# Two transformer blocks on one core: where the differences of the block products are made, the step of residual and norm in out1, and the places and order of down's first loads

## The chip, the core and the metric

One core of a Trainium2 chip runs the whole program. Its engines take their own instruction streams in order and wait for one another by semaphores: TensorE (PE in the views; its weight loads are PEld) multiplies into PSUM banks, VectorE (DVE), ScalarE (ACT) and GpSimd (POOL) work on SBUF, and all but POOL read PSUM; SyncE (SP) issues the transfers. The metric is the device time of one execution in microseconds.

## The reference, cut to what matters

Two blocks on 1024 tokens of width 1024, in float32. The first mixes by a gated recurrence and a stick-breaking attention, the second by two kinds of attention; both end in a gated feed-forward net of 2816 columns and a gate from a per-layer input.

```python
# first block
mix = concatenate([rmsnorm(o_hg, hg_out_norm) * silu(hg), o_sb]) @ w_out
h = h + rmsnorm(mix, attn_post_norm)
u = rmsnorm(h, ffn_pre_norm)
gate, up = split(u @ w_gate_up)
y = (silu(gate) * up) @ w_down
# second block
x = x + y_attention @ w_out
x = x + conv_ffn(rms_norm(x, ffn_norm_g), w_gate, w_up, conv_w, conv_b, w_down)
```

## The kernel before

The program is written with tiles and pools; the framework places the pools and plans the order in which each engine takes its instructions, so that a step may run ahead of one that the code writes before it, if its operands and its place are there. A pool's tiles lie at the address where the pool was opened, one pool behind the other (pools with `side="right"` from the other end), and a tile at an address that an older tile had waits until that one is read for the last time.

**Precision.** Each float32 operand is split into a high part, cast on ScalarE (L219), and a low part, the difference, on VectorE or POOL (L225); a product is three matmuls, high by high, high by low, low by high (`mm3`, L294 to L296; in the block products L1194 to L1196). A token tile is 128 tokens; there are 8.

**Stages around the change.** `out1` (first block) and `out2` (second) make the attention's output per token tile, add the residual, norm, and hand the tile `u_tok` to `put_uT`. `gate_up(s)` then multiplies by the gate's and up's weights, and `down(s)` by those of `w_down`; s is 0 in the first block and 1 in the second.

**out1.** Per tile i, `prep(i)` loads `o`, `gate` and `o_sb`, norms `o` (`norm_u`: square sum on ScalarE, a root in small steps, one step on VectorE, L549) and multiplies by the gate on POOL (L1018); the result is transposed on TensorE. `mm(i, c)` makes the two halves of the output. `fin(i)` norms `y` (L549), adds the residual on POOL (L1044), stores it as `h1` (L1045), and norms again into `u_tok` (square sum, root, L549). Its transposes (L1087) follow behind `mm(i+2)`. `x_res` and `u_tok` share the two buffers of `o_wk`.

**Block products.** `gate_up` uses seven products in place of eight, over a split of weights and tokens in two by two blocks. Tokens: even tiles are the first column of blocks, odd ones the second (`put_uT`: t = i % 2). Products 1 and 2 take B11 and B21, whose parts are made as the even tiles come. The other five take T2 = B22 - T1 (product 6), T1 = B12 - B11 (5), B22 - B12 (7), B21 - T2 (4) and B22 (3), and `right_operands` makes these once all tiles are there, in two halves of 256 columns: differences on POOL and VectorE (L1101), high parts on ScalarE, low ones on VectorE. Their tiles are q-tiles of 8 KB per partition: 8 in `q1` (B blocks and parts of 1 and 2; later those of 4 and one of 3), 7 in `q2`.

**Weights.** `add_pair` loads two raw weight tiles, `raw` and `raw2`, per chain (a 128-column piece of gate or up) and makes four units: the first directly, the second from sums on POOL (L141 to L144, in the one tile `s12`), the third and fourth from what these leave. Four split tiles `w` are live; `pump()` splits the next ones as far as tiles and raw tiles go. The two places of `raw2` are opened in `gate_up`, behind `q2`, so before it the units stop at the first sum.

**The order of products** is `sevens(s, chains)`: for s = 0 products go in pairs of chains 0 and 1; for s = 1 chain 0 goes first with chain 1 pushed in. From chain 2 on products 4 and 3 of a chain come behind product 1 of the next, in both.

**down.** `load(f)` loads a row tile of `act` (L1230) and splits it; `out` adds two rows' products into `y` (L1247). For s = 1 `y` starts as `h3`, loaded in `block1` (L592) ahead of `down`. `act` (4 tiles) is opened ahead of `act_raw` (2 of 4 KB), both from the address where `q1` began.

## Time and profile before

| | us |
|---|---|
| three runs | 2973.06, 2977.28, 2980.13 |
| median | 2977.28 |
| profiled execution | 2983.0 |
| its span, first to last instruction | 2981.2 |
| mean granted clock of TensorE in it | 0.978 of full |

The trace is of the one profiled execution. Busy shares are of the span. "Idle before" is how long an engine had stood still ahead of an instruction and what ended it. A merged line (x3) counts several instructions from the first one's start to the last one's end. The granted clock of a stretch says how far TensorE's clock was at the lower one of its two levels, 1.2 and 2.4 GHz.

### The profile page before, as it was taken

To read this page: it belongs to the slowest core of one execution; us is meant where nothing else is said; L and a number is where in the kernel's file an instruction comes from. 1 tells how busy PE (TensorE), PEld (TensorE's weight loads), DVE (VectorE), ACT (ScalarE), POOL (GpSimd) and SP (SyncE) were. 2 spreads that over 40 slices of the span, in tenths; PEclk is the share of its full clock that TensorE was granted. 3 is DMA by queue.
4 is the path that set the end of the run, shared out by engine and by line. 5 is a ranking of instruction groups with operands and counts; after the bars stand their busy time and mean duration, and the time that the engine had idled before them with its cause. 6 is when DMAs were issued, how large, how long until landed. Compare 5 with 4: busy or idle time off the path is not lost. (4 is left out here: it accounts for less than half of the span.)

```text
span 2981.2 us, 37288 instructions
## 1 busy us (share of the span) xinstructions
PE 2797.0 (94%) x13699; PEld 2295.8 (77%) x13699; DVE 1757.5 (59%) x3120; ACT 1168.8 (39%) x2237; POOL 721.9 (24%) x606
## 2 busy tenths in 40 slices
PE   8989988887999999999999999889979999799999
PEld 6878776765788887887788788767768888588877
DVE  4444687756433333557469775778775555455561
ACT  4121566644333334112246455656443333221131
POOL 1223000035433331222214100020163343122201
PEclk9989999998999999999999999999999999899999
DMA  4212545341322223322235865753322222433221
GB/s 131 67 45 97 156 132 141 116 138 64 92 81 79 83 80 146 106 85 92 69 112 161 215 154 175 198 135 78 124 64 85 81 83 85 158 99 106 75 76 47
DMA packets 277942, 321.36 MB, mean 108 GB/s; under 512 B 14646, under 2 KB 207194, under 8 KB 276222
## 3 DMA queue, kind: packets, MB, share of 16 engines
q1 hardware_dynamic: 277758, 318.97, 35.3%
q8 instruction: 108, 1.77, 0.2%
q14 instruction: 76, 0.62, 0.1%
HBM read 228.69 MB, written 92.59 MB: 108 GB/s over the span
## 5 line engine op out<-in xcount | busy, mean ns | idle before, releaser
L1194 PE MATMUL bank<-q,w 128*128 128x512 f32 x1232 | 484.5, 394 | 32.3 <-ACT w L219 25.5
L1195 PE MATMUL bank<-q,w 128*128 128x512 f32 x1232 | 483.1, 392 | 0.2 <-DVE q L225 0.2
L1196 PE MATMUL bank<-q,w 128*128 128x512 f32 x1232 | 482.1, 392 | 0.0
L219 ACT CAST w<-raw 128x1024 fp32r<-128x1024 f32 (+2 forms) x246 | 236.6, 971 | 532.5 <-DVE y L1247 285.7
L225 DVE TENSOR_TENSOR w<-raw,w 128x1024 fp32r<-128x1024 f32 (+2 forms) x242 | 312.4, 1300 | 134.1 <-ACT w L219 133.3
L1247 DVE TENSOR_TENSOR y<-y,bank 128x512 f32<-128x512 f32 x336 | 227.1, 686 | 171.4 <-PE bank L296 171.3
L294 PE MATMUL bank<-w,act 128*128 128x512 f32 x704 | 276.7, 393 | 26.3 <-ACT act L219 26.3
L1194 PEld LDWEIGHTS bank<-q,w 128*128 128x128 f32 x1232 | 233.7, 190 | 85.0 <-ACT w L219 27.0
L294 PE MATMUL bank<-w,u 128*128 128x512 f32 (+1 forms) x672 | 272.9, 406 | 6.5 <-ACT u L287 3.7
L295 PE MATMUL bank<-w,act 128*128 128x512 f32 x704 | 276.2, 392 | 0.0
L296 PE MATMUL bank<-w,act 128*128 128x512 f32 x704 | 275.8, 392 | 0.1
L1195 PEld LDWEIGHTS bank<-q,w 128*128 128x128 f32 x1232 | 233.3, 189 | 49.3 <-DVE q L225 0.6
L1196 PEld LDWEIGHTS bank<-q,w 128*128 128x128 f32 x1232 | 233.2, 189 | 49.2 <-DVE w L225 0.3
L295 PE MATMUL bank<-w,u 128*128 128x512 f32 (+1 forms) x672 | 266.4, 396 | 2.2 <-POOL w L225 2.0
L296 PE MATMUL bank<-w,u 128*128 128x512 f32 (+1 forms) x672 | 267.6, 398 | 0.0
L225 POOL TENSOR_TENSOR act<-act_raw,act 128x1024 fp32r<-128x1024 f32 x40 | 103.8, 2615 | 332.3 <-ACT act L219 332.3
L294 PEld LDWEIGHTS bank<-w,act 128*128 128x128 f32 x704 | 133.8, 190 | 55.0 <-ACT act L219 27.2
L1134 ACT COPY s<-bank 128x512 f32<-128x512 f32 x132 | 77.4, 588 | 200.7 <-PE bank L1196 200.7
L296 PEld LDWEIGHTS bank<-w,act 128*128 128x128 f32 x704 | 133.2, 189 | 29.2 <-DVE act L225 1.5
L295 PEld LDWEIGHTS bank<-w,act 128*128 128x128 f32 x704 | 133.6, 190 | 27.8
L294 PEld LDWEIGHTS bank<-w,u 128*128 128x128 f32 x672 | 128.0, 191 | 29.7 <-ACT u L287 4.7
L295 PEld LDWEIGHTS bank<-w,u 128*128 128x128 f32 x672 | 128.0, 190 | 25.1 <-POOL w L225 2.9
(360 smaller groups left out, 5571.1 us busy)
## 6 DMA issues: line engine op xcount, KB each, us to landing
raw<-in_w_gate_up_dram SPq DMA_DIRECT2D x44, 512.0 KB
act<-o SPq DMA_DIRECT2D x88, 256.0 KB
raw<-in_w_down_dram SPq DMA_DIRECT2D x44, 512.0 KB
act_raw<-act SPq DMA_DIRECT2D x44, 512.0 KB
raw<-in_w_in_dram SPq DMA_DIRECT2D x40, 512.0 KB
qk<-qkT SPq DMA_DIRECT2D x32, 384.0 KB
raw<-in_w_gate_dram SPq DMA_DIRECT2D x22, 512.0 KB
raw<-in_w_up_dram SPq DMA_DIRECT2D x22, 512.0 KB
```

The lines of the kernel that those rows point to most:

```text
L219: nc.scalar.copy(hi, src)
L225: e.tensor_tensor(lo, src, hi.bitcast(F32), ALU.subtract)
L294: mm(ps, lh, rh, start=start, stop=False)
L295: mm(ps, lh, rl, start=False, stop=False)
L296: mm(ps, ll, rh, start=False, stop=stop)
L1134: nc.scalar.copy(t, src)
L1194: nc.tensor.matmul(ps, w[:, 0, o], uh[:, k, :], start=first_mm, stop=False, skip_group_check=True)
L1195: nc.tensor.matmul(ps, w[:, 0, o], ul[:, k, :], start=False, stop=False, skip_group_check=True)
L1196: nc.tensor.matmul(ps, w[:, 1, o], uh[:, k, :], start=False, stop=k == 3, skip_group_check=True)
L1247: nc.vector.tensor_tensor(y, y, ps, ALU.add)
```

## The change

- **out1**: the gate times `o`, and `y` times its gain (`z`), are made on POOL from what is there before the norm; one VectorE step then multiplies by the root and the other factor, or multiplies and adds the residual. `o_wk` has three buffers.
- **Token differences**: `put_uT` makes T1 from PSUM when an odd tile comes, and B22 - B12 on POOL; for s = 1 also T2 from PSUM, its parts, and B21 - T2 (`behind`). For s = 0 `gate_up` makes T2's in a piece of three pairs and one of one. `right_operands` is left with splits.
- **Places**: for s = 1 T2 and its parts have a pool `q2n`, opened ahead of `out2`, and products 5 and 7 get the places of `out2`'s eight `y` tiles, joined in twos, whose pool now stays open. For s = 0 `raw2` and `s12` lie between two parts of the old `q2`.
- **Weights' sums**: `raw2` and `s12` are opened ahead of `out2` for s = 1, and behind four q-tiles for s = 0.
- **Order**: in `sevens(1)` product 2 of chain 1 comes ahead of product 6 of chain 0, its evacuation behind product 3. In chains 0 and 1 the twelve matmuls of a product go high by high, low by high, high by low.
- **down**: `act_raw` is opened ahead of `act`; the eight loads of `y` are issued behind the first two rows' loads.

```diff
@@ -57,7 +57,7 @@
...
     else:
-        seq = [(0, 1), (0, 2), (1, 1), (0, 6), (0, 5), (0, 7), (0, 4), (0, 3), (1, 2), (1, 6), (1, 5), (1, 7)]
+        seq = [(0, 1), (1, 1), (0, 2), (1, 2), (0, 6), (0, 5), (0, 7), (0, 4), (0, 3), (1, 6), (1, 5), (1, 7)]
         late = [(1, 4), (1, 3)]
@@ -577,19 +577,23 @@
...
         with ExitStack() as cq:
+            yp = self.yp = self.pool("y2", 1, ctx=cq, side="right")
             with ExitStack() as c1:
-                yp = self.pool("y2", 1, ctx=c1, side="right")
-                self.y = [yp.tile([P, D], F32, tag=f"y{i}", name=f"yy{i}") for i in range(NT)]
+                yy = [yp.tile([P, 2 * D], F32, tag=f"y{n}", name=f"yy{n}") for n in range(NT // 2)]
+                self.y = [yy[i // 2][:, (i % 2) * D:(i % 2 + 1) * D] for i in range(NT)]
+                del yy
                 wk = self.pool("t_wk", 2, ctx=c1, side="right")
...
                 self.q1 = self.pool("q1b", 8, ctx=cq)
+                self.qn = self.pool("q2n", 3, ctx=cq)
+                self.open_sums(cq, 1)
                 self.out2(wk)
+                self.y = None
             self.gate_up(1, cq)
...
             self.open_y(c1, 1)
-            for i in range(NT):
-                ld(out=self.y[i], in_=S["h3"][i * P:(i + 1) * P, :])
             self.down(1)
@@ -997,7 +1001,7 @@
...
             Y, OT = {}, {}
-            wk = self.pool("o_wk", 2, ctx=c)
+            wk = self.pool("o_wk", 3, ctx=c)
             gp = self.pool("o_g", 1, ctx=c)
@@ -1014,8 +1018,9 @@
...
                 ld(out=sb, in_=S["osbT"][:, i * P:(i + 1) * P].rearrange("(k p) t -> p k t", p=P))
-                self.norm_u(o, g_hg, o, 512, root=True)
-                nc.gpsimd.tensor_tensor(o, o, gt, ALU.mult)
+                r = self.rstd_sqrt(self.square_sum(o, 512), 512)
+                nc.gpsimd.tensor_tensor(gt, o, gt, ALU.mult)
+                nc.vector.scalar_tensor_tensor(out=o, in0=gt, scalar=r, in1=g_hg, op0=ALU.mult, op1=ALU.mult)
                 OT[i] = u = op.tile([P, 2, 8, P], F32R, tag="oT", name="oT")
@@ -1040,8 +1045,10 @@
...
                 ld(out=x, in_=A["x"][0, i * P:(i + 1) * P, :])
-                self.norm_u(y, g_post, y, root=True)
-                nc.gpsimd.tensor_tensor(y, y, x, ALU.add)
+                z = wk.tile([P, D], F32, tag="u", name="y_g")
+                nc.gpsimd.tensor_tensor(z, y, g_post, ALU.mult)
+                r = self.rstd_sqrt(self.square_sum(y, D), D)
+                nc.vector.scalar_tensor_tensor(out=y, in0=z, scalar=r, in1=x, op0=ALU.mult, op1=ALU.add)
                 ld(out=S["h1"][i * P:(i + 1) * P, :], in_=y)
@@ -1072,10 +1079,31 @@
-    def new_uT(self):
+    def new_uT(self, new=None):
...
         self.uT = {(k, t): self.q(q) for t in range(2) for k in range(2)}
+        self.T2 = None
+        if new is not None:
+            self.new_T2(new)
+    def new_T2(self, new):
+        self.T2 = self.q(new)
+        self.ub[6] = (self.q(new, F32R), self.q(new, F32R))
+    def sub(self, e, out, a, b, c):
+        e.tensor_tensor(out[:, :, c], a[:, :, c], b[:, :, c], ALU.subtract)
+    def behind(self, c, e=None):
+        nc = self.nc
+        if e is not None:
+            self.sub(e, self.T2, self.uT[1, 1], self.uT[0, 0], c)
+        hi, lo = self.ub[6]
+        self.split(hi[:, :, c], lo[:, :, c], self.T2[:, :, c], "act", "dve")
+        self.sub(nc.gpsimd, self.uT[1, 0], self.uT[1, 0], self.T2, c)
@@ -1086,43 +1114,54 @@
...
+            u = self.uT[k, t][:, :, c]
...
-                nc.vector.tensor_copy(self.uT[k, t][:, :, c], v)
+                nc.vector.tensor_copy(u, v)
...
-                nc.scalar.copy(self.uT[k, t][:, :, c], v)
...
-    def right_operands(self, q2):
-        nc = self.nc
-        B11, B12, B21, B22 = (self.uT[n] for n in ((0, 0), (0, 1), (1, 0), (1, 1)))
-        T2 = self.q(q2)
-        sub = lambda e, out, a, b: (lambda c: e.tensor_tensor(out[:, :, c], a[:, :, c], b[:, :, c], ALU.subtract))
-        pool, dve = nc.gpsimd, nc.vector
...
-        for n, pools, value, steps in (
-                (6, (q2, q2), T2, [sub(pool, B11, B12, B11), sub(dve, T2, B22, B11)]),
-                (5, (q2, q2), B11, []),
-                (7, (q2, q2), B12, [sub(pool, B12, B22, B12)]),
-                (4, (self.q1, self.q1), B21, [sub(pool, B21, B21, T2)]),
-                (3, (q2, self.q1), B22, [])):
-            hi, lo = self.ub[n] = tuple(self.q(p, F32R) for p in pools)
+                T1 = self.uT[0, 0][:, :, c]
+                if k == 0:
+                    nc.vector.tensor_tensor(T1, v, T1, ALU.subtract)
+                elif self.T2 is not None:
+                    nc.vector.tensor_tensor(self.T2[:, :, c], v, T1, ALU.subtract)
+                nc.scalar.copy(u, v)
+        if t == 1:
+            if self.T2 is not None:
+                self.behind(c)
+            self.sub(nc.gpsimd, self.uT[0, 1], self.uT[1, 1], self.uT[0, 1], c)
...
+    def right_operands(self, tiles):
...
+        for n, pools, value in ((5, tiles[0:2], (0, 0)), (7, tiles[2:4], (0, 1)),
+                                (4, [self.q1, self.q1], (1, 0)), (3, [tiles[4], self.q1], (1, 1))):
+            hi, lo = self.ub[n] = tuple(p() if callable(p) else self.q(p, F32R) for p in pools)
...
-                for f in steps:
-                    f(c)
-                self.split(hi[:, :, c], lo[:, :, c], value[:, :, c], "act", "dve")
+                self.split(hi[:, :, c], lo[:, :, c], self.uT[value][:, :, c], "act", "dve")
...
+    def open_sums(self, ctx, s):
+        self.W.open_raw("raw2", 2, ctx)
+        self.xp = self.pool(f"s12_{s}", 1, ctx=ctx)
...
-        q2 = self.pool(f"q2_{s}", 7, ctx=ctx)
-        self.W.open_raw("raw2", 2, ctx)
-        self.xp = self.pool(f"s12_{s}", 1, ctx=ctx)
+        if s == 0:
...
+            qa = self.pool("q2a", 4, ctx=ctx)
+            self.open_sums(ctx, s)
+            qb = self.pool("q2b", 3, ctx=ctx)
+            self.W.pump()
+            self.new_T2(qa)
+            for c in (slice(0, 384), slice(384, 512)):
+                self.behind(c, nc.vector)
+            tiles = [qa, qb, qb, qb, qa]
+        else:
+            tiles = [(lambda n=n: self.yp.tile([P, 4, 512], F32R, tag=f"y{n}", name="q")) for n in range(4)] + [self.qn]
...
-        self.W.pump()
-        self.right_operands(q2)
+        self.right_operands(tiles)
@@ -1188,19 +1227,25 @@
...
             w, (uh, ul) = self.W.get(U["p", s, c][unit]), self.ub[n]
-            for k in range(4):
+            parts = [(k, a, b) for k in range(4) for a, b in ((0, 0), (0, 1), (1, 0))]
+            if c < 2:
+                parts = [(k, a, b) for a, b in ((0, 0), (1, 0), (0, 1)) for k in range(4)]
+            for n_mm, (k, a, b) in enumerate(parts):
                 o = slice(half * 512 + k * P, half * 512 + (k + 1) * P)
-                first_mm = bool(first) and k == 0
-                nc.tensor.matmul(ps, w[:, 0, o], uh[:, k, :], start=first_mm, stop=False, skip_group_check=True)
-                nc.tensor.matmul(ps, w[:, 0, o], ul[:, k, :], start=False, stop=False, skip_group_check=True)
-                nc.tensor.matmul(ps, w[:, 1, o], uh[:, k, :], start=False, stop=k == 3, skip_group_check=True)
+                nc.tensor.matmul(ps, w[:, a, o], (uh, ul)[b][:, k, :], start=bool(first) and n_mm == 0,
+                                 stop=n_mm == 11, skip_group_check=True)
             if half == 1 or unit == 3:
...
             elif n == 2:
-                ev(c, 0, 0, ps, x.pop(1))
+                later = lambda: ev(c, 0, 0, ps, x.pop(1))
+                if s == 1 and c == 1:
+                    X["later"] = later
+                else:
+                    later()
             elif n == 6:
@@ -1210,6 +1255,8 @@
...
                 ev(c, 0, 1, ps, x.pop(2))
+                if "later" in X:
+                    X.pop("later")()
             self.W.pump()
@@ -1219,8 +1266,8 @@
...
         with ExitStack() as c:
+            rp = self.pool(f"act_raw{s}", 2, ctx=c)
             actp = self.pool(f"act{s}", 4, ctx=c)
-            rp = self.pool(f"act_raw{s}", 2, ctx=c)
             acts = {}
@@ -1253,6 +1300,9 @@
...
                 load(f)
+            if s == 1:
+                for i in range(NT):
+                    nc.sync.dma_start(out=self.y[i], in_=S["h3"][i * P:(i + 1) * P, :])
             for f0, n in CHUNKS:
@@ -1750,7 +1800,7 @@
...
         self.banks = {"d": [0, 1], "tr": [2, 3]}
-        self.new_uT()
+        self.new_uT(self.qn)
         with ExitStack() as c:
```

## Rows read from the trace of the kernel before

**Rows 1.** The page: busy time, share of the span and instructions of each engine.

```profile
PE 2797.0 (94%) x13699; PEld 2295.8 (77%) x13699; DVE 1757.5 (59%) x3120; ACT 1168.8 (39%) x2237; POOL 721.9 (24%) x606
```

**Rows 2.** Waits of TensorE, whole span: total us, times, longest.

```profile
PE bank L294 <- ACT act L219: 26.3, 2, 20.3
PE bank L1194 <- ACT w L219: 25.5, 3, 12.0
PE bank L282 <- POOL o_hg L1018: 12.4, 5, 3.7
```

**Rows 3.** Table by stretch: length, busy us (instructions) of PE, PEld, DVE, ACT, POOL, clock, DMA share, GB/s.

```profile
586.00:704.90 118.90, 101.14 (x457) 80.70 (x456) 73.89 (x141) 52.64 (x107) 40.11 (x22) 0.97 0.38 129
704.90:760.00 55.10, 35.32 (x129) 27.72 (x127) 38.87 (x40) 25.98 (x37) 34.10 (x15) 0.75 0.22 68
1150.00:1200.00 50.00, 43.28 (x176) 34.70 (x176) 15.57 (x17) 19.45 (x27) 12.51 (x6) 0.90 0.55 197
2100.00:2147.50 47.50, 47.19 (x240) 38.00 (x238) 36.98 (x69) 21.11 (x43) 4.93 (x4) 1.00 0.27 100
2147.50:2165.00 17.50, 12.23 (x56) 9.60 (x56) 14.43 (x16) 7.41 (x12) 11.03 (x4) 0.92 0.29 90
2147.50:2215.00 67.50, 50.72 (x210) 39.60 (x211) 56.31 (x47) 30.04 (x39) 45.65 (x25) 0.90 0.24 74
2250.00:2300.00 50.00, 50.00 (x223) 41.39 (x222) 26.85 (x26) 16.33 (x21) 19.32 (x18) 1.00 0.28 87
2560.00:2660.00 100.00, 78.97 (x333) 64.03 (x332) 47.87 (x58) 23.57 (x26) 14.64 (x8) 0.88 0.41 142
```

**Rows 4.** Timeline, out1 to gate_up(0): start, us, engine, line, operation [idle before, releaser].

```profile
710.81 1.22 PE L1194 MATMUL bank<-q,w 128*128 128x512 f32 x2
...
716.67 4.44 POOL L1044 TENSOR_TENSOR y<-y,x_res 128x1024 f32<-128x1024 f32 x1 [3.51 <-DVE y L549]
...
721.13 0.32 SPq L1045 DMA_DIRECT2D h<-y  x1
...
721.51 1.51 SPq L129 DMA_DIRECT2D raw<-in_w_gate_up_dram  x2
...
724.89 1.57 PE L1087 MATMUL bank<-ident,u_tok 128*128 128x128 f32 x8 [2.28 <-DVE u_tok L549]
...
732.11 2.24 POOL L141 TENSOR_TENSOR s<-raw 128x512 f32<-128x512 f32 x1
...
740.96 0.79 PE L1194 MATMUL bank<-q,w 128*128 128x512 f32 x1 [12.01 <-ACT w L219]
```

**Rows 5.** Timeline, out2 to gate_up(1).

```profile
2166.35 2.24 POOL L141 TENSOR_TENSOR s<-raw 128x512 f32<-128x512 f32 x1
...
2171.06 0.79 PE L1194 MATMUL bank<-q,w 128*128 128x512 f32 x1 [11.27 <-ACT w L219]
```

**Rows 6.** Timeline, gate_up(1) to down(1).

```profile
2598.38 1.61 SPq L1230 DMA_DIRECT2D act_raw<-act  x2
...
2609.72 0.79 PE L294 MATMUL bank<-w,act 128*128 128x512 f32 x1 [20.32 <-ACT act L219]
```

**Rows 7.** Single lines and tiles: count, ns min/median/max, first and last start.

```profile
L549 DVE SCALAR_TENSOR_TENSOR y<-y,rs_y,g_attn_post_norm x8: 1283/1285/3302, 617.9 to 715.3; 128x1024 f32<-128x1024 f32 x8
...
L1018 POOL TENSOR_TENSOR o_hg<-o_hg,gate x8: 1262/1276/2125, 580.5 to 680.6; 128x512 f32<-128x512 f32 x8
...
L1044 POOL TENSOR_TENSOR y<-y,x_res x8: 2367/2391/4438, 620.3 to 716.7; 128x1024 f32<-128x1024 f32 x8
...
L225 DVE TENSOR_TENSOR q<-q x10: 1217/2302/3357, 2158.1 to 2186.8; 128x1024 fp32r<-128x1024 f32 x10
...
L1092 DVE TENSOR_TENSOR q<-bank,q x6: 680/688/692, 2119.6 to 2149.3; 128x512 fp32r<-128x512 f32 x6
...
L592 SPq DMA_DIRECT2D y<-h x8: 423/452/1012, 2589.5 to 2597.2; - x8
```

**Rows 8.** Transfers from 2587 to 2611 us.

```profile
DMA packets 2373, 7.58 MB, mean 316 GB/s; under 512 B 271, under 2 KB 398, under 8 KB 2373
```

## Prediction, made before the result

> **What bounds the kernel now.** TensorE is busy for 94% of the span [rows 1], so time can only come from stretches where it stands still or runs slowly. I read the waits of TensorE next [rows 2]. Two groups lead, 26.3 us at `down`'s products (L294, waiting for `act` rows) and 25.5 us at the block products (L1194, waiting for weight tiles); then 12.4 us in `out1` for `o_hg`. The longest single waits, in the last column, make up most of it: they sit at hand-overs between stages. The table by stretch [rows 3] prices them. A full stretch runs 223 instructions in 50 us, so a 512-column product costs 0.225 us. Multiplying each stretch's count by that (the transposes, 64, 24 and 8 of them, at 0.2 us from the group of 8 that took 1.57 us [rows 4]) gives what each stretch loses to idling and to the lower clock (granted 0.75 of 2.4 GHz in the second):
>
> - `out1`, 118.9 us: 393 x 0.225 + 12.8 = 101; **18 lost**.
> - `out1` to `gate_up(0)`, 55.1 us: 105 x 0.225 + 4.8 = 28; **27 lost** (A).
> - `gate_up(0)` to `down(0)`, 50 us: 176 x 0.225 = 39.6; **10 lost** (B).
> - `out2` to `gate_up(1)`, 67.5 us: 202 x 0.225 + 1.6 = 47; **20 lost** (C).
> - `gate_up(1)` to `down(1)`, 100 us: 333 x 0.225 = 75; **25 lost** (D).
>
> That is 100 us, the most this change can touch. The rest of the kernel keeps its instructions.
>
> **Inside out1.** Per tile the number of instructions stays: one POOL product (`z`, or `gt`) for one POOL sum, one VectorE step for one. What changes is the chain. POOL's 2.39 us add (L1044) and 1.28 us product (L1018) stood behind VectorE's norm [rows 7]; now they run beside ScalarE's square sum. TensorE's five waits for L1018 lose 1.28 us each, 6.4 us; the clock that fell after the longest gives perhaps 1 back. The rest, first weights among it, stays. `z` is a third user of `o_wk`: it waits until the tile two back is transposed, right behind the same `mm`, about a us, which hides under the square sum; without that cover it is a us per tile on a chain with over 10 us of products per tile to hide in. **7 us.**
>
> **A.** Three things end the 12.01 us wait [rows 4], and they go together. First, tile 7's chain: VectorE's norm at 715.3 [rows 7], POOL's add at 716.67 for 4.44 us, the next norm, transposes at 724.89. Without the adds tile 6 is 2.4 us sooner, so tile 7's eviction too; then its own 4.44 us go, and some queueing behind T2: I put the transposes at 716, 9 us sooner. Second, the weights' sums: their second raw tile is loaded at 721.51 because SP stood at tile 7's store (721.13) and because the tile's place belonged to `o_y`; the sums on POOL start at 732.11, behind token differences. In the new order of pools `raw2` lies over `o_in`, whose last tile POOL reads at 680.6 [rows 7], so load and sums (two steps of 2.24 us to the first use) move ahead of the products. Third, T1 goes to VectorE at 0.68 us per pair, read from PSUM [rows 7], and all but the last pair's differences are done before tile 7 comes. TensorE can start its first four products at about 708.4 (710.81 now), and 48 x 0.225 us plus 8 transposes end at 721. VectorE by then owes about 16 us in the 16 us from 704.9: three norms 3.9 at 1.28 with the small steps of their roots, taken as 0.7 each; one eviction and T1 1.4 and tile 6's four steps 2.7 at 0.68; T2 and its low part 4.9, a weight tile 1.2 at 1.22 per 1024 columns; that, not POOL, is late next. I put (0,6) at 723 against 740.96, **18 us**; that the later, smaller waits go is set against VectorE's share of the lock described below. Bounds: 10 (tile 7's chain alone) to 24.
>
> **C.** TensorE runs 48 matmuls (and a tile's 8 transposes) from 2147.5 [rows 3] and then waits 11.27 us for the sums [rows 5], which POOL starts at 2166.35 behind its differences. The moved entry (1,2) in `sevens` is worth nothing: 48 are four products, so the order of execution already has (1,2) ahead of (0,6). With `raw2` open before `out2` the sums are done in time, and T2 and its parts come per pair inside `out2`. The cover is VectorE, busy 37.0 of 47.5 us there [rows 3]. Three pairs add T1, T2 and a low part, 3 x 2.04 = 6.1 us. Until TensorE, unstalled, wants the last operand (eight products and a transpose, 2170), VectorE owes 43.1 + 7.4 (tiles 6 and 7) + 9.8 (eight half operands at 1.22) + 4.3 (weights) + 1.4 = 66 of 70 us. But when POOL works, the same 1.22 us step takes 2.30 us at the median [rows 7]; ten of these are 11 us more, so 7 us of stall appear. With 2 us of slip in `out2` and 2 us of small waits that stay: 20 - 11 = **9 us**. Bounds: 0 and 17.
>
> Those rows show POOL and VectorE stretching each other, 11 us of it in C, which gives the sum of 64 below; were every POOL step there to stop VectorE for its whole length, C would give nothing and the sum 55. The Trainium skill, page "SBUF — State Buffer", section "SBUF: two separate sides", says why this speaks against the change: the two share one port pair under an exclusive lock, held for a whole instruction, for VectorE steps with two SBUF inputs. The rows agree: 1217 ns alone, 3357 at most, and the steps that read PSUM stay at 680 to 692. By that rule moving POOL's subtractions beside `out2` buys a place, not time, as in the second rival below.
>
> **B and D.** `down`'s first rows lay at the place of `q1`'s fifth tile, an operand of the last two products; at offset 0 they lie over the operand of product 1, whose last use is seven products (19 us) before the end. Rows 0 and 1 were written long ago, so loads, casts and low parts (1.22 us) fit into the tail; around it VectorE is busy for 48 of 100 us and ScalarE for 24 [rows 3]. In B the whole 6.0 us wait (26.3 less 20.3 [rows 2]) goes with its low clock: 10 less 1 that stays, **9 us**. In D eight `y` loads of 512 KB stood ahead of the rows on SP (issued from 2589.5 to 2597.2 [rows 7], the rows at 2598.38, 20.32 us of wait [rows 6]). Now they are behind them, each of two row loads passing eight `y` loads. Late next is `y` itself: six banks let TensorE run 8 us before the first sum must be done, then it needs one `y` per 2.7 us; at the 316 GB/s moved there [rows 8] one takes 1.7 us. So: 25 less 1 that stays and 3 for a first `y` that waits for the last `o` store, **21 us**. Grouping products by high and low parts for c < 2 adds nothing and lets a late low part pass; I cost it at nothing, worth under 1.8 us per product.
>
> **Sum.** 7 + 18 + 9 + 9 + 21 = 64. The profiled execution took 2983.0 us (span 2981.2), so 2919; the median shown is 2977.3, 0.2% lower, so **2913**.
>
> **Rivals.** (1) Rows not early: SP takes in order, and if the row loads stay behind the last `act` stores, B keeps its 6 us and D falls to such a wait: 7 + 18 + 0 + 9 + 14 = 48, 2929. For it: at 721.13 SP held weight loads behind a store in just this way [rows 4]. Against: the order of execution isn't that of the code; block products run from 710.81 on, ahead of tile 7's transposes, though the code writes them behind [rows 4], so steps go where their place comes free. (2) VectorE takes over: the lock costs A down to 10, C to 0, `out1` to 3: 43 us, 2934. For it: 66 of 70 us. (3) All stalls close: 84 us, 2893; against it speaks the same figure. (4) **Slower**: POOL's queue. It takes in order; if both sums of A (8 steps, 16 us at about 2 us) are planned ahead of `z` of tiles 6 and 7, those 16 us enter their chain: A loses 16. In C, if all POOL work in `out2` (8 differences at 1.26 and 16 us of sums, 26) blocks VectorE, which has 10.5 - 6.1 = 4 us to spare, it loses 22. With nothing in `out1` and B, D as forecast: +38 - 30 = +8, 2985. It decides only if A's sums stand ahead of tile 6's `z`. Against it: POOL is busy for 40 of 119 us in `out1` [rows 3], so both find room one after the other.
>
> **Chances.** Forecast 0.52 (own range 2901 to 2925), (1) 0.15, (2) 0.20, (3) 0.10, (4) 0.03. About 0.2% is what a measurement here can tell from no change. Only (4) is not faster; part of it lies within 0.2%: faster 0.97, same 0.01, slower 0.02. The range takes in (1), (2) and (3): 2893 to 2938.
>
> **What would show it.** Right: no wait over 3 us at the first `down` products, `act_raw` loads issued before the last block product; the wait for `w` at L1194 gone and L141 ahead of tile 7's transposes; in C a few us of waits for `q`, with VectorE at over 90% from 2100 on. Wrong: a wait for `act` above 5 us (1), waits of TensorE for `q` from VectorE adding to over 15 us (2), or for `u_tok` behind POOL (4). An order that moves stalls into stages the change doesn't name would make the whole sum wrong.

## The result, and the profile after

| | before | after |
|---|---|---|
| median, us (4 runs each, side by side) | 2976.3 | 2926.8 |
| lowest to highest | 2973.1 to 2980.1 | 2924.5 to 2928.5 |
| ratio, 95% interval | | 0.9833, 0.9815 to 0.985 |
| profiled execution / its span | 2983.0 / 2981.2 | 2926.4 / 2924.6 |

The change takes 49.5 us; the forecast was 64, and rival (1) gave 48. The page line on busy time, to be read against [rows 1]:

```profile
PE 2785.4 (95%) x13699; PEld 2283.7 (78%) x13699; DVE 1757.2 (60%) x3132; ACT 1169.3 (40%) x2239; POOL 700.6 (24%) x608
```

The number of matmuls is the same; the span lost 56.6 us and TensorE's busy time 11.6, so most of the gain is standing still that went away, and the rest a clock that fell less often. Where it went is seen by cutting the span at TensorE's own instructions. The table gives the us between them in the profiled executions, worked out from the first starts and the last ends in each trace:

| stretch | before | after | change | forecast |
|---|---|---|---|---|
| first product of out1 to its last | 117.9 | 112.2 | -5.7 | -7 |
| to the last of gate_up(0) (A) | 451.7 | 436.0 | -15.7 | -18 |
| to the last of down(0) (B) | 248.9 | 249.3 | +0.5 | -9 |
| to the first of out2 | 686.7 | 676.0 | -10.8 | 0 |
| to the last of gate_up(1) (C) | 497.2 | 489.0 | -8.2 | -9 |
| to the last of down(1) (D) | 263.3 | 248.4 | -14.9 | -21 |
| ahead of out1, and behind down(1) | 715.5 | 713.6 | -1.9 | 0 |

The stretch from down(0) to out2 needs a word: every engine has the same instructions there in both kernels, TensorE's in the same order and the others' in the same but for a few neighbours. Over all fourteen profiled executions told of here it took between 676.0 and 686.7 us. The two ends are these two kernels, but the kernel before with another order of loads behind it (e4) took 681.2, and the changed kernel in another execution (e1) 685.2, so its 10.8 us can't be put down to the change; the profiled execution of before, 6.7 us above its median, was a long one. The five stretches that the change touches give -44.0 us. The medians give 5.5 us more, which no run assigns.

TensorE's waits after, against [rows 2] (us in total, times, longest):

```profile
PE bank L294 <- ACT act L219: 13.1, 4, 5.7
PE bank L1115 <- DVE rs_a L257: 9.0, 1, 9.0
...
PE bank L282 <- DVE rs_a L257: 3.6, 1, 3.6
...
PE bank L282 <- DVE q L1122: 2.3, 1, 2.3
PE bank L1236 <- DVE q L1121: 1.7, 1, 1.7
...
PE bank L1236 <- ACT w L219: 1.3, 1, 1.3
```

The wait for `w` at the block products (L1236, which was L1194) fell from 25.5 to 1.3 us, the waits for POOL's `o_hg` are gone (at the same transposes, L282, two are left, 3.6 and 2.3 us, which VectorE ends), and 20.3 us for `act` became 5.7. But a second 5.7 us, at down(0), is where it was, and the wait at tile 6's transposes (L1115) has grown to 9.0 us from 3.28. The stretches, against [rows 3] (same columns):

```profile
585.92:698.16 112.24, 102.83 (x450) 82.10 (x451) 79.39 (x142) 53.20 (x106) 44.54 (x27) 0.94 0.45 143
698.16:760.00 61.84, 50.75 (x227) 41.49 (x226) 47.17 (x52) 33.50 (x48) 33.10 (x20) 0.92 0.26 80
1100.00:1150.00 50.00, 42.52 (x174) 33.24 (x173) 19.34 (x18) 17.16 (x23) 5.25 (x6) 0.93 0.43 151
2059.50:2116.93 57.43, 55.39 (x277) 44.06 (x277) 51.29 (x97) 28.79 (x52) 11.45 (x9) 1.00 0.40 134
2500.00:2600.00 100.00, 92.95 (x397) 74.81 (x396) 54.04 (x64) 26.28 (x30) 22.98 (x15) 0.97 0.46 159
```

The hand-over of out1 to gate_up(0) runs at a clock of 0.92 of full, where it was 0.75; that of gate_up(0) to down(0) is as poor as before (174 instructions in 50 us; 176 before), and VectorE is busy for 89% of out2 (51.3 of 57.4 us). How the new 9.04 us come about, from the timeline (start, us, engine, line, operation [idle before, releaser]):

```profile
696.06 2.21 POOL L141 TENSOR_TENSOR s<-raw 128x512 f32<-128x512 f32 x1 [3.21 <-issue]
...
698.34 1.26 POOL L142 TENSOR_TENSOR s<-s,raw 128x512 f32<-128x512 f32 x1
...
699.64 1.04 ACT L219 CAST w<-s 128x1024 fp32r<-128x1024 f32 x1 [3.58 <-POOL s L142]
700.59 1.05 ACT L267 ACTIVATE junk<-y 128x1024 bf16<-128x1024 f32 x1
...
706.64 1.28 DVE L549 SCALAR_TENSOR_TENSOR u_tok<-y,rs_y,g_ffn_pre_norm 128x1024 f32<-128x1024 f32 x1
...
708.07 1.94 PE L1115 MATMUL bank<-ident,u_tok 128*128 128x128 f32 x8 [9.04 <-DVE rs_a L257]
...
709.81 3.51 POOL L1097 TENSOR_TENSOR q<-q 128x1536 f32<-128x1536 f32 x1 [3.22 <-DVE rs_y L261]
...
710.42 3.98 DVE L1051 SCALAR_TENSOR_TENSOR y<-y_g,rs_y,x_res 128x1024 f32<-128x1024 f32 x1
```

The sums (L141, L142) are ahead of tile 7, as forecast, but also ahead of tile 6: ScalarE's next instruction is the cast of the second sum, and it stands for 3.58 us until POOL has made it. Tile 6's square sum (L267) has its place behind that cast. The last two lines belong to e9. Then come tile 7's transposes and, behind the wait for the last piece of its operand's high part, the first product 6, (0,6):

```profile
719.94 1.07 PE L1115 MATMUL bank<-ident,u_tok 128*128 128x128 f32 x8 [1.14 <-DVE u_tok L549]
...
726.07 1.20 PE L1236 MATMUL bank<-q,w 128*128 128x512 f32 x4 [0.91 <-ACT q L219]
```

And the hand-over to down(0), which did not improve:

```profile
1133.90 0.33 SPq L111 DMA_DIRECT2D raw<-in_w_down_dram  x1
...
1134.29 0.42 SPq L1277 DMA_DIRECT2D act_raw<-act  x1
...
1136.40 0.32 SPq L1220 DMA_DIRECT2D act<-o  x1
...
1137.86 0.46 SPq L1277 DMA_DIRECT2D act_raw<-act  x1
...
1138.78 1.04 ACT L219 CAST act<-act_raw 128x1024 fp32r<-128x1024 f32 x1 [3.50 <-DMA act_raw<-act]
...
1139.88 0.80 PE L294 MATMUL bank<-w,act 128*128 128x512 f32 x1 [5.67 <-ACT act L219]
```

The first row is asked for (L1277) at 1134.29 us, as the last block product ends (1134.20), right behind a load of down's weights (L111) that had to wait for its own raw tile. It goes ahead of the last store of `act` (L1220). Its place had been free for long: product 1 of the last chain, the last reader of that operand, stands eight products, 96 matmuls or some 22 us, ahead of the end.

### The profile page after: what moved, and what is told of

Its sections match the earlier page's. It is cut to its first block, busy times and chain, and to the rows that moved or that the text cites. A ratio compares the mean times of both kernels' runs of the same rounds, so it can differ in the third digit from the quotient of the medians.

```text
span 2924.6 us, 37294 instructions
## 1 busy us (share of the span) xinstructions
PE 2785.4 (95%) x13699; PEld 2283.7 (78%) x13699; DVE 1757.2 (60%) x3132; ACT 1169.3 (40%) x2239; POOL 700.6 (24%) x608
## 5 line engine op out<-in xcount | busy, mean ns | idle before, releaser
L1236 PE MATMUL bank<-q,w 128*128 128x512 f32 x3696 | 846.1, 391 | 6.0 <-DVE q L1121 1.7
L1236 PEld LDWEIGHTS bank<-q,w 128*128 128x128 f32 x3696 | 693.2, 188 | 157.7 <-ACT s L1173 2.4
L1173 ACT COPY s<-bank 128x512 f32<-128x512 f32 x132 | 77.5, 588 | 204.2 <-PE bank L1236 204.2
L294 PEld LDWEIGHTS bank<-w,u 128*128 128x128 f32 x672 | 127.9, 190 | 30.0 <-ACT u L287 5.4
L295 PEld LDWEIGHTS bank<-w,u 128*128 128x128 f32 x672 | 127.8, 190 | 25.4 <-POOL w L225 3.2
L296 PEld LDWEIGHTS bank<-w,u 128*128 128x128 f32 x672 | 127.8, 190 | 24.8
L225 DVE TENSOR_TENSOR w<-s,w 128x1024 fp32r<-128x1024 f32 x44 | 54.3, 1233 | 138.4 <-ACT w L219 138.3
L861 DVE TENSOR_TENSOR at<-bank,at 128x512 fp32r<-128x512 f32 (+1 forms) x160 | 99.8, 628 | 39.7 <-ACT at L860 38.8
L141 POOL TENSOR_TENSOR s<-raw 128x512 f32<-128x512 f32 x44 | 59.3, 1348 | 229.5 <-DVE w L225 149.6
```

The lines of the kernel that those rows point to most:

```text
L141: pool(x[:, HI], r2[:, LO], r2[:, HI], ALU.add)
L225: e.tensor_tensor(lo, src, hi.bitcast(F32), ALU.subtract)
L294: mm(ps, lh, rh, start=start, stop=False)
L295: mm(ps, lh, rl, start=False, stop=False)
L296: mm(ps, ll, rh, start=False, stop=stop)
L861: nc.vector.tensor_tensor(at[:, 1, 0:w], ps[:, 0:w], at[:, 0, 0:w].bitcast(F32), ALU.subtract)
```

## Experiments: when the rows of down come

All e-runs are told against the changed kernel's 2926.8 us and its stretches. Times of one kernel differ between executions by some us, most of it in the stretch named above, so the stretches decide.

**e1, e3, e4.** Theory 1 was that the order of execution gives a place to a new tile only when the pool that held it has been closed, and `q1` is closed behind the last product. e1 keeps a part of `q1` open through `down` and takes the first rows' tiles from it:

```diff
-        with ExitStack() as cq:
-            self.q1 = self.pool("q1", 8, ctx=cq)
+        cr = ExitStack()
+        self.q1 = self.pool("q1", 5, ctx=cr)
+        with ExitStack() as cq:
+            self.qs = self.pool("q1s", 3, ctx=cq)
...
         for c, n in sevens(s, NF):
             product(c, n)
+            if (c, n) == (NF - 1, 2):
+                self.first_rows()
...
+    def first_rows(self):
+        rr = self.q(self.q1).rearrange("p a t -> p (a t)")
+        self.acts = {}
+        for f in range(2):
+            r = rr[:, f * T:(f + 1) * T]
+            self.nc.sync.dma_start(out=r, in_=self.S["act"][f * P:(f + 1) * P, :])
+            a = self.acts[f] = self.q1.tile([P, 2, T], F32R, tag="q", name="act")
+            self.split(a[:, 0], a[:, 1], r, "act", "dve")
```

> The changed kernel, with down's first two row tiles in places of the q1 pool, which stays open through down: the raw rows lie in the place of B22, which is read for the last time when product 3's operand is split, and the two act tiles in those of product 1's operand. The loads are written behind product 2 of the last chain. Theory 1 (a place comes free for the planner only when the pool that had it is closed, which is behind the last product): now the rows are loaded long ahead and split in the tail, and TensorE's waits of 5.67 us at down(0) and 5.71 us at down(1) fall under 1 us each; 9 to 11 us less than the changed kernel's 2926.8, so 2916 to 2918. Theory 2 (the rows come late because ScalarE and VectorE are taken up with the last products): the waits stay at 3 to 5 us and the time within 4 us of 2926.8.

Measured: 2916.6 us (0.979, 0.9776 to 0.9804), 10.2 less. No wait for `act` is left among TensorE's; the rows' loads (first and last start below) go out as soon as the rows are written, some 380 us earlier than in the changed kernel.

```profile
L1279 SPq DMA_DIRECT2D q<-act x4: 319/320/532, 750.0 to 2171.4; - x4
```

The stretch to down(0)'s end fell from 249.3 to 238.5 us: 10.9, twice the 5.7 us wait, since the clock no longer falls behind it: 1.00 in 1100 to 1150 us, against 0.93 in the same stretch above (same columns).

```profile
1100.00:1150.00 50.00, 50.00 (x222) 41.29 (x221) 18.83 (x18) 24.07 (x34) 11.89 (x7) 1.00 0.45 153
```

At down(1) only 2.3 us came (248.4 to 246.1). There the next thing was late, `y`:

```profile
2551.47 6.71 SPq L1320 DMA_DIRECT2D y<-h  x8
...
2559.23 3.25 DVE L1311 TENSOR_TENSOR y<-y,bank 128x512 f32<-128x512 f32 x5 [8.66 <-DMA y<-h]
...
2559.97 0.79 PE L295 MATMUL bank<-w,act 128*128 128x512 f32 x1 [5.16 <-DVE y L1311]
```

Theory 1 holds for the rows. e1 also writes their loads earlier in the code, but behind product 2 of the last chain, 60 matmuls ahead of the end; loads that go out 380 us sooner didn't get their time from that line. Which edit then made the 14.9 us at down(1)? e3 undoes both edits of `down` in the changed kernel (the reverse of the two hunks in front), e4 puts them alone into the kernel before.

> The changed kernel with both edits of down undone: act opened ahead of act_raw, and the eight y loads written ahead of down(1). Theory 1 (these two edits made the gain at down(1)): the wait there goes back from 5.71 to about 20.3 us, 14 to 15 us slower than the changed kernel, 2941. Theory 2 (the y tiles now lie over gate_up(1)'s own tiles, which are read to its end, so their loads go behind the rows whatever order they are written in): the wait stays at 5.7 us, the time at 2927.

> The kernel before with the two edits of down alone. Both theories of the other run allow a gain here; it tells whether the edits can do it by themselves: the wait at down(1) falls from 20.32 to 5.7 us, 14 to 15 us less than 2976.3, 2962, if the order of the eight loads against the rows is what counts. If the place of the y tiles is what counts, nothing changes. At down(0) 6.0 us stay in either case, as the rows' places are not given out before the last product.

The same group of waits, in e3 and then in e4:

```profile
PE bank L294 <- ACT act L219: 12.3, 4, 5.9
```

```profile
PE bank L294 <- ACT act L219: 11.5, 2, 5.8
```

e3: 2930.1 us (0.9836, 0.9822 to 0.985), down(1)'s stretch 248.6 for 248.4: nothing. e4: 2964.3 us, 13.0 less than the kernel before (0.9952, 0.9935 to 0.9969), the stretch 248.4 for 263.3, all 14.9. So the two edits can move the rows ahead of the eight `y` loads by themselves, and in the changed kernel they aren't needed: the loads have the same order in e3 without them. The likely reason is the place of `y`: with `y2` kept open and four q-tiles fewer on the left, the `y` tiles of down(1) now lie over the sums' tile and gate_up(1)'s own, which are read to the end, where they lay over `q2`. That is read from the addresses; no run moved these tiles alone. In both kernels the 5.7 us stay, as in B.

**e5.** From e1's `y`: the eight tiles get the places of the `y2` pool, kept open, that is those of products 5 and 7, whose last uses are 3 and 2 products ahead of the end. The padding of e2 (below) is in it too.

```diff
+        cy = ExitStack()
         with ExitStack() as cq:
-            yp = self.yp = self.pool("y2", 1, ctx=cq, side="right")
+            yp = self.yp = self.pool("y2", 1, ctx=cy, side="right")
...
+            yy = [self.yp.tile([P, 2 * D], F32, tag=f"y{n}", name="y") for n in range(NT // 2)]
+            self.y = [yy[i // 2][:, (i % 2) * D:(i % 2 + 1) * D] for i in range(NT)]
```

> The kernel of e1 with two more steps: the 32 bytes of e2, and y of down(1) in the places of the y2 pool, which now stays open to the end, so that y0 to y3 lie where product 5's operand lay and y4 to y7 where product 7's lay. Theory 1 (in e1 the y loads, issued at 2551.5 us behind the last products, took the place of the rows: TensorE waited 5.16 us for the first sum): with places in an open pool they are issued after the last use of 5 and 7, some 8 and 5 us before the end; the 5.16 us go, and the padding takes 4 us: 2916.6 - 5 - 4 = 2907 to 2908. Theory 2 (the eight loads only pass what is late next, the w_down tiles and the last stores on SP): another wait of 2 to 5 us comes in down(1), 2911 to 2913.

Measured: 2903.5 us (0.9748, 0.9733 to 0.9762), 23.3 less than the changed kernel and the fastest of all. down(1)'s stretch is 239.7 us, 6.5 less than in e1, with no wait for `y` or `act`; gate_up(1)'s 485.6, 4.4 less; 1.6 us came behind down(1), which no theory said. At this point both hand-overs into `down` are closed.

## Experiments: the places of products 5 and 7

Nothing in the forecast said that gate_up(1) would run more slowly, but it does. TensorE's row of a table by stretch from 2200 to 2500 us, where it is busy throughout (length, busy us, instructions, clock, DMA share, GB/s), in the changed kernel and then in e2:

```profile
2200.00:2500.00 300.00, 300.00 (x1312) 1.00 0.26 82
```

```profile
2200.00:2500.00 300.00, 300.00 (x1325) 1.00 0.26 82
```

A chain of seven products took 19.24 us where gate_up(0), and gate_up(1) of the kernel before, take 19.04. By the starts of ScalarE's copies (L1173; L1174 in e2) nearly all of the excess is in one place: from the copy of product 6 to that of 7, with products 5 and 7 in it, 5.58 us in the mean in place of 5.41. One chain's two copies, in the changed kernel and then in e2:

```profile
2305.68 0.59 ACT L1173 COPY s<-bank 128x512 f32<-128x512 f32 x1 [1.46 <-PE bank L1236]
...
2311.23 0.59 ACT L1173 COPY s<-bank 128x512 f32<-128x512 f32 x1 [0.73 <-PE bank L1236]
```

```profile
2306.01 0.59 ACT L1174 COPY s<-bank 128x512 f32<-128x512 f32 x1 [1.46 <-PE bank L1237]
...
2311.39 0.59 ACT L1174 COPY s<-bank 128x512 f32<-128x512 f32 x1 [0.65 <-PE bank L1237]
```

Their four tiles are the ones from `y2`, at 196576 bytes and up, 32 over a multiple of 64; all other tiles of operands begin at a multiple of 64. e2 moves them by 32 bytes:

```diff
+            self.pool("pad", 1, ctx=cq, side="right").tile([P, 8], F32, name="pad")
             yp = self.yp = self.pool("y2", 1, ctx=cq, side="right")
```

> The changed kernel with 32 bytes per partition kept free at the right end of SBUF, so that the places of products 5 and 7 in gate_up(1) begin at a multiple of 64 bytes like those of all other operands (196544 in place of 196576). Theory 1 (an operand that begins 32 bytes off a multiple of 64 is read more slowly): the pair of products 5 and 7 falls from 5.58 to 5.40 us, a chain of gate_up(1) from 19.24 to 19.04 us, and the kernel becomes 4 us faster, 2922 to 2923. Theory 2 (it is the place at the far end, or what else reads there): 19.24 us stays, no change.

Measured: the pair took 5.41 us, a chain 19.04, out2 to gate_up(1)'s end 484.8 us for 489.0: 4.2 less. By the whole time 2925.3 (0.982, 0.9804 to 0.9836) it can't be told from the changed kernel, the stretch that differs between executions having taken 5 us more; by its own stretch, and by the 4.4 us of e5, it is shown. The chain takes 19.04 us in all five runs with the 32 bytes (e2, e5, e9, e10, e12) and 19.24 in the seven others of the changed kernel.

## Experiments: out1's step, the sums, and tile 6

**e7** puts out1's old steps (norm, then POOL's product and sum, two buffers) back, **e8** the old places of `raw2` and `s12`, in both blocks.

```diff
-                self.open_sums(cq, 1)
...
-            self.open_sums(ctx, s)
             qb = self.pool("q2b", 3, ctx=ctx)
+            self.open_sums(ctx, s)
...
         else:
+            self.open_sums(ctx, s)
+            self.W.pump()
```

> The changed kernel with out1's steps as before: norm, then the gate's product and the residual on POOL, two buffers of o_wk. Theory 1 (the new step takes 5 waits of TensorE for POOL's product, 1.1 to 1.3 us each, and 2.4 and 4.4 us off tiles 6 and 7): the last product of out1 comes 118 us after the first in place of 112, tile 6's transposes and the block products 4 to 6 us later: 2932 to 2937. Theory 2 (what out1 gains is lost at once in the wait for tile 6, which the sums set): out1's last product comes 6 us later, but the first block product at most 1 us: 2927 to 2930.

> The changed kernel with raw2 and s12 opened where they were, behind all the q-tiles and inside gate_up, for both blocks. Theory 1 (the early place of the sums made the gain at both block products): in gate_up(1) TensorE waits 8 to 11 us for the sums after the first four products, in gate_up(0) 8 to 12 us; 16 to 22 us slower than the changed kernel, 2943 to 2949. Theory 2 (VectorE's work on the operands is late anyway, so that the sums are half hidden by it): 2 to 5 us in each, 2931 to 2937.

Waits of TensorE in e7, and then in e8:

```profile
PE bank L1112 <- DVE u_tok L549: 14.5, 4, 9.7
PE bank L282 <- POOL o_hg L1022: 10.5, 4, 3.7
```

```profile
PE bank L1237 <- ACT w L219: 17.7, 3, 9.7
PE bank L1114 <- DVE u_tok L549: 2.8, 2, 2.6
...
PE bank L1114 <- ACT q L1128: 2.1, 1, 2.1
```

e7: 2945.4 us (0.9883, 0.9867 to 0.99). out1's products take 119.4 us for 112.2, and up to gate_up(0)'s last it is 559.1 for 548.3: the new step is worth 10.8 us, 7.2 inside out1 and 3.6 behind it (tile 7). By the profiled executions 8.1 of the other us lie in the stretch that differs between them (684.1), and 2.6 at down(1), which no run explains. e8: 2944.0 us (0.9884, 0.9865 to 0.9902). The same stretch takes 556.7, 8.4 more, and out2 to gate_up(1)'s end 492.9 for 489.0, 3.9 more. So in gate_up(0) the early sums are worth what was said, and in gate_up(1) half: the product there waits 5.63 us for the sum, not 11; why not more wasn't tried. e8 shows the price of the early sums too: without them TensorE waits 2.1 us at tile 6, not 9.04. (out1's products end 2.8 us sooner, but that stretch, 109.5 us here, took from 108.6 (e11) to 112.2 us (the changed kernel) where no edit concerns it.)

**e6, e9, e10** try to have both. e6 puts the second `raw2` tile where tile 7's `oT` lies, so that its sum can't go ahead of tile 6; e9, on e5, takes the piece of three pairs off POOL's path, by making B21 - T2 once, behind the last pair; e10 is both. The edit of e9:

```diff
     def behind(self, c, e=None):
...
+        if e is not None:
+            if c.stop < 512:
+                return
+            c = slice(0, 512)
         self.sub(nc.gpsimd, self.uT[1, 0], self.uT[1, 0], self.T2, c)
```

> The changed kernel with the second raw2 tile of gate_up(0) in the place of tile 7's oT in place of gate's, so that the second chain's sums can't be planned before out1's last product; the rest of the order stays as near as may be. Theory 1 (the cast of the second sum, planned on ScalarE ahead of tile 6's square sum and held there until 699.64 us by POOL, makes tile 6 late by 3.5 us): TensorE's wait of 9.04 us at tile 6's transposes falls to 5 or 6, 3 to 4 us less, 2923. Theory 2 (VectorE's queue, with the sum of tile 7's second half and the differences, sets tile 6): 8 to 9 us stay, or the time comes back as a wait of product 6 of chain 1 for the sum: within 1 us of 2926.8.

> The kernel of e5 with product 4's difference B21 - T2 of gate_up(0) made in one step of 512 x 4 columns behind the last pair, in place of one piece of three pairs and one of one; so POOL has no such step beside tile 7's chain. Theory 1 (the piece, 3.51 us on POOL, held VectorE's step of residual and norm for tile 7, 3.98 us in place of 1.27): that step takes 1.3 us again, tile 7's transposes come 2 to 3 us sooner and so does everything behind: 2903.5 - 2.5 = 2901. Theory 2 (tile 7's chain has other queues to wait in): no change, 2903 to 2904.

> The kernel of e9 with the second sum later, as in e6. There tile 6 came 6 us sooner and tile 7 waited 6.58 us, while POOL made the piece of three pairs in 6.27 us and VectorE took 3.3 us to get from one 0.68 us step to the next. Theory 1 (it was that piece that gave e6's gain back): without it both tiles come early, TensorE's waits at the two tiles are under 5 us together in place of 10, and the time is 3 to 6 us under e9's, 2895 to 2898. Theory 2 (POOL's sums, once beside the differences, hold VectorE as the piece did): waits of over 5 us come for tile 7 or for the second sum, and the time is 5 to 10 us over e9's, 2906 to 2911.

e6, timeline:

```profile
702.66 0.63 PE L1119 MATMUL bank<-ident,u_tok 128*128 128x128 f32 x4 [1.85 <-DVE u_tok L553]
...
705.61 6.27 POOL L1101 TENSOR_TENSOR q<-q 128x512 f32<-128x512 f32 x2
...
714.74 2.31 DVE L1055 SCALAR_TENSOR_TENSOR y<-y_g,rs_y,x_res 128x1024 f32<-128x1024 f32 x1
...
724.69 1.73 PE L1119 MATMUL bank<-ident,u_tok 128*128 128x128 f32 x7 [6.58 <-DVE u_tok L553]
```

Tile 6 is 6 us sooner (the wait is 1.85 us), so the second sum, which now comes later, was what held it: the square sum starts 0.1 us behind tile 6's step of residual, where it had waited 3.5 us for the cast, and two small steps of VectorE behind it take 0.22 and 0.16 us in place of 1.35 and 1.18. But now tile 7's step of residual (L1055) starts at 714.74 and its transposes wait 6.58 us; out1's first product to gate_up(0)'s last takes 553.4 us for 548.3, the whole 2938.6 (0.9861, 0.9847 to 0.9876); 8.2 us more than in the changed kernel lie in the stretch that differs between executions. Theory 1 was right on the cause and wrong on the worth: the time comes back, with interest, at the next tile.

e9: the step that took 3.98 us takes 1.28, and tile 7's `u_tok` is made 4 us sooner, counted from out1's first product, than in the changed kernel:

```profile
708.21 1.28 DVE L1065 SCALAR_TENSOR_TENSOR y<-y_g,rs_y,x_res 128x1024 f32<-128x1024 f32 x1
```

Yet the stretch is 547.8 us (e5: 547.9), since TensorE then waits 2.33 us for the low part of the next late operand:

```profile
PE bank L1254 <- DVE q L226: 2.3, 1, 2.3
```

The whole is 2907.8 us (0.9773, 0.9758 to 0.9788), no gain. e10: TensorE's waits at the two tiles are 8.2 us together, then 2.6 and 1.7 for operands; 551.5 us, 3.7 more than e9; 2910.0 (0.9779, 0.9765 to 0.9794). Theory 1's number didn't come; theory 2's range did, but not its 5 to 10 us over e9 (2.2 came), and the wait at tile 7 is 4.70 us. What is shown is that each relief on the way from out1 to gate_up(0) uncovers the next queue, VectorE's above all; none of the four other orders (e6, e8, e9, e10) took that stretch below the changed kernel's by more than repeats differ (546.6 to 548.3 us in the changed kernel, e1, e2, e3 and e5).

## Experiments: the order of the products

e11 is the changed kernel with the old `sevens(1)`, the old place of the evacuation and the old order of the twelve matmuls; e12 is e5 with the grouping for gate_up(1) only (`if c < 2 and s == 1`).

> The changed kernel with the order of its products as before: the old list in sevens(1), product 2's evacuation of chain 1 in its place, and high by high, high by low, low by high per piece in all chains. The prediction put both at nothing. If that holds, every stretch stays within 1 us, 2926 to 2929. If the grouping lets a late low part pass, the waits of the first products at each hand-over grow by up to 1.8 us each: 2929 to 2934.

> The kernel of e5 with the twelve matmuls of a product in chains 0 and 1 of gate_up(0) in their old order, high by high, high by low, low by high per piece; gate_up(1) keeps the new one. In e11, where both had the old order, out1's first product to gate_up(0)'s last took 545.5 us, against 548.3 in the changed kernel and 546.6 to 547.9 in e1, e2, e3 and e5, which share its order there. Theory 1 (grouping by high and low parts costs in gate_up(0), since a product then wants a whole high part before it can begin its low one): 545.5 again, 2 us less than e5's 547.9, 2901 to 2902. Theory 2 (the grouping is worth nothing there, and 545.5 lies within what repeats differ by): 547 to 548, 2903 to 2905.

e11: 2933.8 us (0.9865, 0.9846 to 0.9883); out2 to gate_up(1)'s end 491.6 us, 2.6 more than the changed kernel, out1's stretch 545.5, 2.8 less. e12: 2906.7 us (0.9767, 0.9749 to 0.9784), the stretch 548.0 us as in e5. So 545.5 lay within what repeats differ by and the grouping is worth nothing in gate_up(0); in gate_up(1), where repeats lie between 488.8 and 490.0, the new order is worth about 2 us. Grouping and list weren't told apart there.

## Why the prediction was right, and where not

- **As a whole.** 2913 was forecast, with an own range of 2901 to 2925; 2926.8 lies outside that and inside the whole range, which took in the rivals, 2 us from rival (1), which had a chance of 0.15 against the forecast's 0.52. The signs named for A came: the wait for `w` fell to 1.3 us, and L141 stands ahead of tile 7's transposes. Those named for `down` failed at both places: waits of 5.67 and 5.71 us for `act`, and row loads behind the last block product.
- **out1, 7 us: right.** 5.7 in the comparison, 7.2 by e7. POOL's product behind the norm was the cause; five waits for `o_hg`, 12.4 us, became two, 5.9 us, that VectorE ends.
- **A, 18 us: right in sum** (15.7), with one step wrong. The wait for `w` went, as the sums moved ahead, which e8 prices at 8.4, and tile 7's chain gave 3.6 (e7). But "load and sums (two steps of 2.24 us to the first use) move ahead of the products" was taken as free. Their cast stands in ScalarE's queue ahead of tile 6, so the transposes of tile 7 came at 719.9 us, not 716, and (0,6) at 726.1, not 723. Rival (4) named this kind of delay, for POOL's queue and at 16 us; it was ScalarE's, behind POOL, and 7 us (9.04 against 2.1). The clock paid some of it back: 1.00 from 720 us on, where before it was still at 0.93 from 741 to 800 us.
- **C, 9 us: right by two errors.** 8.2 came, but 4.2 us of cost nobody had forecast are in it (the 32 bytes), so the hand-over itself gained 12.4. The term that was too large is "ten of these are 11 us more": the small waits around the first products add to 5.5 us (0.74, 1.72, 1.80 and 1.28, and no longer one), and VectorE was busy for 89% and 83% of the two halves (51.3 of 57.4 us, 39.9 of the 48.1 behind), not above 90%. Of the gain the sums are 3.9 (e8), the order of products 2 (e11), which had been put at nothing. The other 6 or so are left to the differences and their places, which no run put back alone; what they are worth by themselves is not shown, here or in A.
- **B, 9 us: wrong, 0 came. D, 21 us: 14.9 came.** This is rival (1) as priced, 0 and 14. The step that failed is "Rows 0 and 1 were written long ago, so loads, casts and low parts (1.22 us) fit into the tail". The place was free even earlier than said, eight products ahead and not seven. But a place in a pool that isn't open yet can't be asked for, and the new pool opens only when the old one has closed, behind the last product. The evidence used against the rival, that products run ahead of transposes the code writes earlier, was of tiles in open pools, and so said nothing on this. Nor was it quite the rival's mechanism: the first load went ahead of the last `act` store (1134.29 against 1136.40 us), so what held it was the place, not the store. In D there was a second step: the first `y` was put at 3 us, and e1, with the rows in time, waits 5.16 us for it. e1 and e5 turn it into a gain: 10.9 in B, 8.7 in D.
- **D's cause** was half right: the rows' place ahead of eight `y` loads is the gain (e4), but the edits of `down` are not what secures it in the changed kernel (e3).
- **Rival (2)**, VectorE under the lock, didn't come: C gave 8.2, not 0. What the prediction calls the lock is in the trace: tile 7's step, 1.27 us for tile 6, took 3.98 and ended 1.1 us behind the POOL step that had begun before it (710.42 + 3.98, against 709.81 + 3.51). The Trainium skill, page "SBUF — State Buffer", section "SBUF: two separate sides", says that of VectorE and GpSimd whichever starts first has the shared port pair for the whole instruction; these rows agree. What e9 adds is that taking the collision away gained nothing, since TensorE's next operand was late by as much.
- **The sum.** 64 forecast; 44 in the five stretches, 49.5 by the medians. Of the missing 20, 15.6 are the hand-overs into `down` (9.5 in B, 6.1 in D, where the rows alone give 2.3 of it and the rest takes `y`), 2.3 A, 1.3 out1 and 0.8 C, where the 4.2 us for the 32 bytes ate what the hand-over gave beyond the forecast.

## What to carry to other kernels

A transfer can't start before its tile has a place, and under a planner a place is more than a free address: if the old owner's pool is still open the load waits for the pool, so tiles that must come early belong in a pool that spans both stages. When a step is moved ahead, look at each queue it now stands in front of; the cast of a sum that nobody needs yet can hold the norm that everybody waits for. When a stall is closed, name the next late thing and close that too: here the rows alone gave 2.3 us at down(1), and with `y` 8.7.

## What the runs showed of the hardware

A matmul whose moving operand begins 32 bytes off a multiple of 64 in SBUF ran slower: 24 of them in 5.58 us in place of 5.41, 3%, at a full clock and with no wait; 32 bytes of padding took it away (e2, e5). Only these two places were tried, and only this shape (128x512). The Trainium skill, page "SBUF — State Buffer", section "Operand start alignment", asks only that an operand start at a multiple of its element size, and says that it speaks of legality, not of speed; the runs here add the speed.
